# Sixteen modulation vectors of layer 1, computed in the FFN's down stage and not in layer 0's last attention heads

## The chip, the cores and the metric

The kernel runs on one core of one Trainium2 chip. The metric is the device time of one execution in microseconds (us), as a median over several runs. The core has five engines that run side by side: TensorE (PE, with its weight loads as PEld), VectorE (DVE), ScalarE (ACT), GpSimd (POOL) and SyncE (SP, which here only issues transfers). They wait for each other by semaphores.

## What is computed

The reference is a network of two layers over 512 latent tokens and 256 context tokens of width 1024. Layer 0 mixes tokens by multi-head latent attention with 8 heads, layer 1 by a gated linear recurrence with 8 heads. A SwiGLU FFN of width 2816 follows each. Every sub-layer is normalised and then shifted, scaled and gated by modulation vectors:

```
def modulate(x, shift, scale):
    return x * (1 + scale) + shift

def swiglu(a, w1, w3, w2):
    return (jax.nn.silu(a @ w1) * (a @ w3)) @ w2
```

The modulation is a product of SiLU(c), for the latent and for the context tokens, with a weight matrix of each layer: 48 vectors of 128 values a layer. In the kernel four of them make a group, named here by its first vector; groups 0, 4, 8 and 12 of layer 1 hold the shift and scale of its first norm.

## The kernel before

All arithmetic is float32. Where accuracy counts, a value is split into a high and a low part, and a product takes three matmuls: high by high, high by low, low by high (`mm3`, L96 to L102, rows L100, L101 and L102 of the trace). A weight tile is loaded to a buffer `wf`, ScalarE casts its high part (`wh` or `sh`) and VectorE or GpSimd subtracts the low part (`wl`, `sl`).

The program is written once in program order. A scheduler then sets the order of each engine's instructions, with priorities for named pieces of work (`PRIO`); the piece `ada_m` has the priority −500, so its instructions fill places that the others leave.

**The modulation.** `ada(l, u0, n, pool, bank)` (L153 to L171) computes n vectors of layer l from vector u0 on. For each it takes a buffer of the ring and lets SP load 512 KB of weights into it (L158), and TensorE runs eight matmuls of 32 columns (L161):

```
w = self.ring.tile([P, RING], F32, tag="wf", name="adaw", bufs=4)
nc.sync.dma_start(out=w[:, :D], in_=self.a["ADA"][l, u0 + i])
```

A group of four is so 32 matmuls (each is two instructions in the trace), one copy of the result by ScalarE (`rows`, L164), four transposes by TensorE (L167), and a small reduction and an addition by VectorE (L169, L171). The ring with the tag `wf` has four buffers, and all weight loads of the program share them, in program order.

**The attention heads.** `mla_attend` (from L430) runs the eight heads of layer 0. A head projects its queries, keys and values with a weight WUP, then runs six blocks of queries: the scores of one block (L517 to L521), the maximum (L524), the exponential (L527), six transposes (L533), and the values for each pair of blocks. Behind each head stand the groups that the table `ADA_HEAD` gives for it (L544), where numbers from 48 on are layer 1's. Behind the heads come three column tiles of the out-projection, with the weight MWO.

**The FFN's down stage.** `ffn_down_first` (L739) multiplies by W2 with Strassen's scheme: seven products in the place of eight. The inner dimension goes in three chunks (`CHUNKS`) of 4, 4 and 3 tiles. Each chunk has four turns (c = 0 to 3), and each turn two column tiles of the result. A turn loads two pieces of W2 (L748), forms sums of them (`sa`, `sb`) and their high and low parts, runs seven products of 12 matmuls with 384 columns (84 in the first two chunks), and adds the results to the residual. In a chunk's last turn the operands of the next chunk are loaded (`d`, L735, from ScalarE's queue) and split (`op`). The text names the four turns of the second chunk B, C, D and E. TensorE's results go to banks named `L` (two), `M` (one) and `q` (five); `self.big` hands out L, L, M in rotation.

Behind layer 0's FFN `norm_scale(1, 0)` (L312) reads the sums of groups 0 to 12.

Of the kernel before, what the change touches and what calls it, by code (L numbers as in the profile page):

```python
# [41 lines left out]
BC_LEN = 1024  # L42
RING = 1024
BT = 3
ADA_HEAD = ((), (16,), (20,), (), (24,), (28,), (32, 36), (48, 52, 56, 60))
ADA_HG = ((), (), (), (), (), (), (), (24, 28, 32))
ADA_O = (36,)
KEEP, CUTS, SB, GSB = (0, 11), (0, 2), (4, 4), (0, 9)
# [10 lines left out]
class Kernel:  # L59
# [370 lines left out]
    def mla_attend(self, es):  # L430
# [10 lines left out]
        for h in range(H):  # L441
# [61 lines left out]
            with self.at("m_att" if h < H - 1 else "m_last"):  # L503
                for q0, nq, k0, k1 in ((0, 2, 0, TT), (2, 2, 0, TT), (4, 2, 4, TT)):
# [37 lines left out]
                    else:  # L542
                        self.split(os[h][0][:, qs], os[h][1][:, qs], ov, nc.vector)
            for u in ADA_HEAD[h]:  # L544
                with self.at("ada_m"):
# [193 lines left out]
    def ffn_down_first(self, l, x, segs, hn, ops, gd, fs, ps, ft, st, spool, acc):  # L739
        nc = self.nc  # L740
        for ci, (p0, p1) in enumerate(CHUNKS):
            m = p1 - p0
            last = ci == len(CHUNKS) - 1
            for c in range(KD // 2):
                raw = []
                for k in (c, c + KD // 2):
                    w = self.ring.tile([P, RING], F32, tag="wf", name="wf", bufs=4)
                    nc.sync.dma_start(out=w[:, :2 * m * P], in_=self.a["W2"][l, k, :, 2 * p0 * P:2 * p1 * P])  # L748
                    raw.append(w)
                after = None  # L750
                if c == KD // 2 - 1 and not last:
                    after = lambda t: self.down_operand(t, gd[ci + 1], ops, ft)
                y = st()
                self.strassen(raw, m * P, y, ops[:m], fs, ps, DOWN_DVE, after)
                yv = y.rearrange("p a b -> p (a b)").rearrange("p (a b) -> p a b", a=2)
                for i, k in enumerate((c, c + KD // 2)):
                    self.residual(x, k, [yv[:, i, c0:c1] for _, c0, c1 in segs], self.mod[l][:, 40 + k, :], segs,
                                  spool if last else None, acc if last else None)
# [433 lines left out]
```

## Time and profile before

| | us |
|---|---|
| median of three runs | 1838.24 (1836.86 to 1839.51) |
| the profiled execution | 1838.41 |
| its span, first to last instruction | 1836.3 |
| mean granted clock of TensorE, full speed is 1 | 0.978 |

A profile shows one execution. The busy share of an engine is the time in which it has an instruction, over the span. In a timeline row the columns are start, duration, engine, line, operation, result and inputs with their shape, and the number of instructions; a bracket holds the idle time of the engine just before and what ended it. A row of waits holds the engine and line that waited, what it waited for, the sum in us, how often, and the longest. Where instructions of an engine overlap in a pipeline, the distance of two starts is the cost, not the duration.

### The profile page before, as it was taken

The numbers are of one execution on the slowest core, as the hardware profiler recorded it, in microseconds if no ns is written. First come the engines' busy times: TensorE is split into PE (matmuls) and PEld (weight loads), VectorE is DVE, ScalarE is ACT, GpSimd is POOL, SyncE is SP. The second block draws the span as 40 slices with busy tenths as digits, with TensorE's granted clock in tenths as the row PEclk, the third lists the DMA queues.
The fourth block names the chain that finished last, engine by engine and source line by source line (L and its number), as shares of the span: only waits on it lengthen the run. The fifth ranks groups of instructions, "written<-read, shape, count | busy, mean of one in ns | idle before, by whom it ended". The sixth has DMA issues, their size and how long they took to land. (4 is left out here: it accounts for less than half of the span.)

```text
span 1836.3 us, 33260 instructions
## 1 busy us (share of the span) xinstructions
PE 1740.9 (95%) x13576; PEld 1594.1 (87%) x13576; DVE 1186.0 (65%) x1916; ACT 815.6 (44%) x1597; POOL 705.0 (38%) x496
## 2 busy tenths in 40 slices
PE   4989999999899999999998999999998889999999
PEld 3878988778799999999996888888886779999888
DVE  5566897741765656598897666575745278888400
ACT  4455565532544444454454332433333265555411
POOL 2343342216566666620004554555543440000442
PEclk9999999999999999999997999999999999999999
DMA  8411032423233433364434121111115333333331
GB/s 274 134 49 65 24 117 98 170 77 122 104 115 126 146 123 121 113 198 146 147 119 163 47 69 48 60 57 59 59 36 196 103 128 114 97 112 104 112 116 49
DMA packets 64391, 198.14 MB, mean 108 GB/s; under 512 B 6640, under 2 KB 18800, under 8 KB 64240
## 3 DMA queue, kind: packets, MB, share of 16 engines
q1 hardware_dynamic: 61216, 180.90, 29.7%
q10 hardware_dynamic: 3024, 15.14, 2.6%
q8 instruction: 106, 1.74, 0.4%
q14 instruction: 45, 0.37, 0.1%
HBM read 178.77 MB, written 17.24 MB: 107 GB/s over the span
## 5 line engine op out<-in xcount | busy, mean ns | idle before, releaser
L87 POOL TENSOR_TENSOR wl<-wf,wh 128x1024 fp32r<-128x1024 f32 (+3 forms) x98 | 228.4, 2337 | 346.7 <-ACT wh L86 339.5
L100 PE MATMUL q<-op,sh 128*128 128x384 f32 (+1 forms) x816 | 257.1, 317 | 4.8 <-ACT op L631 2.5
L101 PE MATMUL q<-op,sh 128*128 128x384 f32 (+1 forms) x816 | 256.9, 316 | 0.0
L102 PE MATMUL q<-op,sl 128*128 128x384 f32 (+1 forms) x816 | 254.2, 317 | 0.5 <-DVE sl L626 0.5
L86 ACT CAST wh<-wf 128x1024 fp32r<-128x1024 f32 (+3 forms) x98 | 97.9, 1001 | 165.1 <-PE L L101 78.0
L100 PEld LDWEIGHTS q<-op,sh 128*128 128x128 f32 x816 | 153.8, 189 | 6.8 <-ACT op L631 3.1
L101 PEld LDWEIGHTS q<-op,sh 128*128 128x128 f32 x816 | 153.8, 189 | 0.0
L102 PEld LDWEIGHTS q<-op,sl 128*128 128x128 f32 x816 | 152.9, 188 | 0.8 <-DVE sl L626 0.8
L625 ACT CAST sh<-wf 128x1024 fp32r<-128x1024 f32 (+1 forms) x104 | 85.5, 823 | 86.5 <-PE L L101 37.2
L100 PE MATMUL L<-op,sh 128*128 128x384 f32 (+1 forms) x368 | 118.2, 321 | 3.0 <-ACT sh L625 3.0
L197 POOL TENSOR_TENSOR acc<-acc,sq 128x512 f32<-128x512 f32 (+1 forms) x30 | 35.3, 1177 | 218.2 <-ACT sq L193 218.2
L102 PE MATMUL L<-op,sl 128*128 128x384 f32 (+1 forms) x368 | 117.8, 320 | 0.1
L101 PE MATMUL L<-op,sh 128*128 128x384 f32 (+1 forms) x368 | 117.7, 320 | 0.0
L626 POOL TENSOR_TENSOR sl<-wf,sh 128x1024 fp32r<-128x1024 f32 (+1 forms) x40 | 90.3, 2258 | 61.2 <-ACT sh L625 61.2
L1121 DVE TENSOR_TENSOR X<-X,T 128x512 f32<-128x512 f32 x96 | 78.2, 856 | 48.9 <-PE lv L1046 45.4
L625 ACT CAST sh<-sb 128x1024 fp32r<-128x1024 f32 (+1 forms) x52 | 53.7, 1033 | 95.4 <-PE q L101 51.5
L100 PE MATMUL L<-f_hi,wh 128*128 128x512 f32 (+1 forms) x232 | 86.3, 372 | 0.0
L101 PE MATMUL L<-f_lo,wh 128*128 128x512 f32 (+1 forms) x232 | 85.8, 370 | 0.0
L102 PE MATMUL L<-f_hi,wl 128*128 128x512 f32 (+1 forms) x232 | 85.4, 368 | 0.0
L625 ACT CAST sh<-sa 128x1024 fp32r<-128x1024 f32 (+1 forms) x52 | 53.7, 1034 | 54.6 <-PE q L101 39.8
L100 PE MATMUL M<-op,sh 128*128 128x384 f32 (+1 forms) x244 | 75.9, 311 | 0.0
L102 PE MATMUL M<-op,sl 128*128 128x384 f32 (+1 forms) x244 | 75.7, 310 | 0.0
(475 smaller groups left out, 5364.1 us busy)
## 6 DMA issues: line engine op xcount, KB each, us to landing
wf<-in_W SPq DMA_DIRECT2D x120, 512.0 KB, 3.6
adaw<-in_ADA SPq DMA_DIRECT2D x96, 512.0 KB, 4.4
wf<-in_HW SPq DMA_DIRECT2D x32, 512.0 KB, 3.5
d<-gd ACTq DMA_DIRECT2D x14, 768.0 KB, 5.2
gd<-s SPq DMA_DIRECT2D x11, 768.0 KB, 4.3
wf<-in_W SPq DMA_DIRECT2D x16, 384.0 KB, 3.2
gd<-s SPq DMA_DIRECT2D x11, 384.0 KB, 2.8
wf<-in_MWO SPq DMA_DIRECT2D x8, 512.0 KB, 4.3
```

The source lines that it names most:

```text
L86: nc.scalar.copy(hi[:, :n], w[:, :n])
L87: nc.gpsimd.tensor_sub(lo[:, :n], w[:, :n], hi[:, :n].bitcast(F32))
L100: nc.tensor.matmul(out, lhsT=lh, rhs=rh, start=(new and i == 0), stop=False, skip_group_check=more)
L101: nc.tensor.matmul(out, lhsT=lh, rhs=rl, start=False, stop=False, skip_group_check=more)
L102: nc.tensor.matmul(out, lhsT=ll, rhs=rh, start=False, stop=(i == n - 1), skip_group_check=more)
L197: (eng or nc.gpsimd).tensor_add(acc[:, c0:c1], acc[:, c0:c1], sq[:, :n])
L625: nc.scalar.copy(hi[:, :n], s)
L626: (nc.vector if j in on_dve else nc.gpsimd).tensor_sub(lo[:, :n], s, hi[:, :n].bitcast(F32))
L1121: nc.vector.tensor_tensor(v, v, t, op=ALU.mult)
```

## The change

Layer 1's groups 0, 4, 8 and 12 (48 to 60 in the table) leave the list of the last head. They are computed in the four turns of the down stage's second chunk, one group a turn, after the turn's Strassen products in program order, with no priority of their own (the name `ada_m` is not used there) and with `self.big` for their banks. In the table group 36 of layer 0, which stood behind head 6 with group 32, moves behind the last head.

```
-ADA_HEAD = ((), (16,), (20,), (), (24,), (28,), (32, 36), (48, 52, 56, 60))
+ADA_HEAD = ((), (16,), (20,), (), (24,), (28,), (32,), (36,))
+ADA_DOWN = (0, 4, 8, 12)
...
                 self.strassen(raw, m * P, y, ops[:m], fs, ps, DOWN_DVE, after)
                 yv = y.rearrange("p a b -> p (a b)").rearrange("p (a b) -> p a b", a=2)
+                if ci == 1:
+                    self.ada(1, ADA_DOWN[c], 4, fs, self.big)
```

What it moves on the engines is seen in the order of their instructions. Each row is a line of the program, the operation, its result and inputs, the shape and how many stand in a row. In the changed kernel lines have numbers higher by one, behind L756 by three; here by one.

ScalarE in head 5, where the norm of the next head's projections ends (`lg`, `y`) and the copy of a group stands (`rows`). Before:

```order
L527 ACTIVATE p,rsum<-sc,nm 128x768
L242 ACTIVATE lg<-ss,eps 128x9
L244 ACTIVATE y<-lg 128x9
L164 COPY rows<-L 128x512
L493 CAST qk_hi<-M 128x3x128
L541 COPY oT<-ov 128x256
L535 CAST pt_hi<-tp_3505 128x6x128
L527 ACTIVATE p,rsum<-sc,nm 128x768
L86 CAST wh<-wf 128x512
```

And after:

```order
L528 ACTIVATE p,rsum<-sc,nm 128x768
L243 ACTIVATE lg<-ss,eps 128x9
L87 CAST wh<-wf 128x512
L245 ACTIVATE y<-lg 128x9
L165 COPY rows<-L 128x512
L494 CAST qk_hi<-M 128x3x128
L542 COPY oT<-ov 128x256
L536 CAST pt_hi<-tp_3505 128x6x128
L528 ACTIVATE p,rsum<-sc,nm 128x768
```

The cast of the 512-column WUP weight has moved ahead, from behind the second exponential to ahead of `y`.

SP in the down stage, with the stores of the up stage's last result and then the loads of W2. Before:

```order
L748 DMA wf<-in_W 128x1024
L728 DMA gd_5438<-s 128x4x384
L748 DMA wf<-in_W 128x1024 x9
L748 DMA wf<-in_W 128x768 x8
L85 DMA wf<-in_HW 128x1024 x2
```

And after:

```order
L749 DMA wf<-in_W 128x1024 x3
L159 DMA adaw<-in_ADA 128x1024 x4
L749 DMA wf<-in_W 128x1024 x2
L159 DMA adaw<-in_ADA 128x1024 x4
L749 DMA wf<-in_W 128x1024 x2
L159 DMA adaw<-in_ADA 128x1024 x4
L749 DMA wf<-in_W 128x1024 x2
L159 DMA adaw<-in_ADA 128x1024 x4
L749 DMA wf<-in_W 128x768 x8
```

Between the two loads of one turn and those of the next stand now four loads of modulation weights.

TensorE at the end of turn D, with the last products of the turn (`q`) and the first of turn E behind them. Before:

```order
L100 MATMUL q<-op_5453,sh 128x384
L101 MATMUL q<-op_5453,sh 128x384
L102 MATMUL q<-op_5453,sl 128x384
L100 MATMUL L<-op_5450,sh 128x384
L101 MATMUL L<-op_5450,sh 128x384
L100 MATMUL q<-op_5450,sh 128x384
L101 MATMUL q<-op_5450,sh 128x384
```

And after:

```order
L101 MATMUL q<-op_5249,sh 128x384
L102 MATMUL q<-op_5249,sh 128x384
L103 MATMUL q<-op_5249,sl 128x384
L162 MATMUL M<-adaw,s_79 32x128 x27
L168 MATMUL L<-ident,rows 128x128 x4
L101 MATMUL L<-op_5246,sh 128x384
L102 MATMUL L<-op_5246,sh 128x384
L101 MATMUL q<-op_5246,sh 128x384
L102 MATMUL q<-op_5246,sh 128x384
L103 MATMUL L<-op_5246,sl 128x384
```

27 of the group's 32 matmuls and its transposes stand in one piece between the two turns.

## Rows read from the trace of the kernel before

**Rows 1.** The page, part 1: busy us of each engine, share, instructions.
```profile
PE 1740.9 (95%) x13576; PEld 1594.1 (87%) x13576; DVE 1186.0 (65%) x1916; ACT 815.6 (44%) x1597; POOL 705.0 (38%) x496
```

**Rows 2.** Window: length, PE, PEld, DVE, ACT, POOL, PEclk, DMA share, GB/s.
```profile
860.00:880.00 20.00, 19.92 (x114) 19.60 (x112) 20.00 (x37) 14.16 (x29) 0.00 (x0) 1.00 0.53 176
```

**Rows 3.** Timeline of PE, a later stage with modulation fragments among matmuls.
```profile
974.34 0.34 PE L102 MATMUL M<-op,sl 128*128 128x384 f32 x1
974.61 0.62 PE L161 MATMUL L<-adaw,s 128*32 128x128 f32 x10
...
975.44 0.34 PE L101 MATMUL L<-op,sh 128*128 128x384 f32 x1
...
977.03 0.34 PE L101 MATMUL q<-op,sh 128*128 128x384 f32 x1
977.29 0.42 PE L161 MATMUL L<-adaw,s 128*32 128x128 f32 x6
...
977.92 0.34 PE L101 MATMUL M<-op,sh 128*128 128x384 f32 x1
```

**Rows 4.** Waits of PE from 301 to 395 us: total, times, longest.
```profile
PE L L161 <- DMA adaw<-in_ADA: 1.0, 1, 1.0
PE sc L517 <- ACT p L527: 0.5, 1, 0.5
PE L L167 <- ACT rows L164: 0.4, 1, 0.4
PE L L100 <- DVE v_lo L470: 0.3, 1, 0.3
PE ov L101 <- DVE pt_lo L536: 0.2, 1, 0.2
```

**Rows 5.** DMA issues from 225 to 365 us: number, KB, us to landing.
```profile
wf<-in_MWO SPq DMA_DIRECT2D x4, 512.0 KB, 4.8
wf<-in_WUP SPq DMA_DIRECT2D x2, 256.0 KB, 2.9
```

**Rows 6.** Timelines of SP and ACT in head 5.
```profile
305.09 2.84 SPq L158 DMA_DIRECT2D adaw<-in_ADA  x4
306.25 0.21 ACT L244 ACTIVATE y<-lg 128x9 f32<-128x9 f32 x1
306.88 0.59 ACT L164 COPY rows<-L 128x512 f32<-128x512 f32 x1 [0.42 <-PE L L161]
```

**Rows 7.** The page, part 6: landing of a W2 load.
```profile
wf<-in_W SPq DMA_DIRECT2D x120, 512.0 KB, 3.6
```

**Rows 8.** Timelines of ACT and DVE in the down stage: a weight's high and low part.
```profile
898.57 1.05 ACT L625 CAST sh<-wf 128x1024 fp32r<-128x1024 f32 x1 [1.10 <-PE M L101]
899.65 1.23 DVE L626 TENSOR_TENSOR sl<-wf,sh 128x1024 fp32r<-128x1024 f32 x1
```

**Rows 9.** Timelines of PE, DVE and ACT in the last head.
```profile
390.54 0.39 PE L517 MATMUL sc<-qk_hi 128*128 128x512 f32 x1
392.46 0.96 DVE L524 TENSOR_REDUCE nm<-sc 128x1 f32<-128x768 f32 x1 [1.99 <-PE sc L521]
393.46 0.90 ACT L527 ACTIVATE p<-sc,nm 128x768 f32<-128x768 f32 x1 [3.97 <-DVE nm L524]
396.94 0.38 PE L517 MATMUL sc<-qk_hi 128*128 128x256 f32 x1 [1.11 <-ACT p L527]
```

**Rows 10.** Waits of SP's queue from 830 to 960 us.
```profile
SPq L748 <- DVE sl L626: 94.5, 13, 13.9
```

**Rows 11.** Waits of all engines from 860 to 945 us.
```profile
ACT op L631 <- DMA d<-gd: 12.0, 8, 4.0
...
PE L L100 <- ACT sh L625: 1.2, 2, 1.0
...
PE q L100 <- ACT op L631: 1.0, 1, 1.0
...
PE q L100 <- ACT s L830: 0.7, 1, 0.7
```

## The prediction

> **What bounds the kernel now.** I read five views, in this order: the engines' shares, the windows by stage, TensorE's waits in the two stretches that the change touches, the timelines there, and the DMA landings. The first shows PE busy for 95% of the span [rows 1], so the time is PE's own work plus the little it waits. The second asks what stands beside PE where work arrives. In the down stage PE is busy for 19.92 of 20 us and VectorE for 20.00 of 20 [rows 2]: there is no hole to fill, and 114 matmuls in 19.92 us make 0.175 us each, so one turn of 84 matmuls takes 14.7 us. In the heads the change takes work away from a chain (score, maximum, exponential, transposes, values) that has its own length. So the question is: how much of the work's time do the heads give back once it is gone, and does the down stage take all of it on top? My numbers stand in lines of the kernel before; the changed file is one line longer from L45 on, three from L757 on.
>
> The profiled execution took 1838.41 us, with a span of 1836.3 and 2.1 outside it, which the change doesn't touch. It lies 0.17 us above the median of the three runs (1838.24), so I add to it directly.
>
> **What the moved work costs PE.** One group is 32 program matmuls of 32 columns (64 in the trace), whose weights are a quarter of the array high, then four transposes. The scheduler cuts a group into fragments between other matmuls. Three rows of the same kind, in a later stage, price a fragment [rows 3]. From the last 384-column matmul ahead of the x10 fragment (974.34) to the second one behind (975.44) are 1.10 us; two matmuls are 0.35, so the fragment costs 0.75. The x6 one costs 977.92 − 977.03 − 0.35 = 0.54. The four instructions more, which begin one more set of eight, make 0.21 to 0.22. So I price a fragment at 0.32 plus 0.222 for each set of up to eight trace instructions. The order of the kernel before has the four groups in 18 fragments with 39 sets, which is 5.8 + 8.7 = 14.4 us. The changed order has them in 20 fragments with 39 sets, 6.4 + 8.7 = 15.1 us. The 16 transposes cost the same in both places and are left out. Group 36, which ran in five fragments of 9 sets, becomes one of 8 in the head after: 4 × 0.32 + 0.22 = 1.5 us less.
>
> **What the heads give back.** Removed: 14.4 + 1.5 = 15.9. The PE waits of 301 to 395 us sum to 2.4 [rows 4]; they come from the old places and I let them all go. New idle time stands against these 18.3:
> (a) ScalarE. In the changed order the cast of the 512-column WUP weight stands ahead of `y` (L244), which the next head's transposes follow. SP no longer issues the x4 of 305.09 for group 36 there, and the WUP load takes the place of the first of them. Landed in 2.9 [rows 5], cast in about 0.6 (ScalarE's copy of the rows, of the same size, took 0.59 [rows 6]), it is ready at 308.6, where `y` began at 306.25. So the chain is 2.3 late, and nothing else stands ready for PE: 2.3.
> (b) The first out-projection weight. Its buffer is released only by group 36's matmuls, which now run in the head after. From these to the first matmul that wants it PE has about 3.0 us of work. The landing is between the 3.6 of a W2 load [rows 7] and the 4.8 that these took among the old ada loads [rows 5]; I take 4.0, nearer the free one, and the 1.05 cast [rows 8]: 2.0. Three weight casts now stand ahead of an exponential on ScalarE, which wait with it: 1.1 more. Together 3.1.
> (c) The scores. A score's buffer is free once the exponential of the one before has read it. From the score at 390.54 its maximum begins at 392.46, the exponential at 393.46 for 0.90: about 4.0 us from score to score, and where less work stands between, PE waits (1.11 at 396.94) [rows 9]. In the changed order of the last two heads three pairs have only 2.1, 3.2 and 3.1 us of matmuls between them, which the fill used to make up: 1.9 + 0.8 + 0.9 = 3.6.
> Sum of the new idle time 9.0, so the heads give back 18.3 − 9.0 = 9.3 us. Bounds: if none of (a) to (c) shows, 18.3; if each is half as large again and the old waits stay, 15.9 − 13.5 = 2.4. I take the middle, because each comes from a row of the same chain.
>
> **What the down stage takes.** The four turns B to E of the second chunk (from 868 on) each get one group.
> Its PE time: 15.1, all of it on the path, since PE there has next to no idle time. From below: if the 0.32 of a switch is hidden there, 8.7.
> ScalarE's copy of the rows stands between the last matmul and the transposes: 0.59 [rows 6]. In turn D nothing is left to cover it, because all 27 remaining matmuls and the transposes close the turn: 0.7. In the other turns matmuls of the turn cover it, and without these each would cost the same 0.7.
> SP's queue. The four ada loads are queued between one turn's W2 loads and the next's, in one ring of four buffers. SP waited 94.5 us in 13 waits for these buffers before [rows 10], which means the W2 loads came as early as the ring allows, two turns ahead. With four more buffers used in each turn they come one turn ahead. Behind each waiting ada load stands the next turn's W2. In turns B, C and E its buffers come free early enough. In D they come free inside the burst of 27: behind the third of these matmuls stand 24, 1.33 us, then transposes 0.44, the copy 0.7, and four matmuls of the next turn 0.7 before the first that needs the low half: 3.2 us. The load needs 3.6 to land, the cast 1.05, the low half 1.23 [rows 7, 8]: 5.9. So PE waits 2.7 in turn E. From below 0, if the buffer is released before the burst; from above 5.9.
> What the old waits give: 1.0 and the larger part of 1.2 in turn B, where PE waited for a cast and an operand, now have ada matmuls to run: −2.0. The 0.7 of the stage's end goes the same way [rows 11]: −0.7.
> VectorE and ScalarE get four small reductions, additions and copies, under 4 us in all, beside their 20.00 of 20; I cost them at nothing, because PE is what the turn waits for; if VectorE became the bound it would be 1.5.
> Sum: 15.1 + 0.7 + 2.7 − 2.0 − 0.7 = 15.8 (bounds 8.7 − 2.7 = 6 and 15.1 + 2.8 + 5.9 = 23.8). Behind it norm_scale of layer 2 reads the groups' sums; group 12 ends in turn E, with the four turns of the third chunk still to come, so nobody waits for it.
>
> **Net.** Unrounded, 15.76 − 9.32 = +6.4: 1838.41 + 6.4 = 1844.8 us.
>
> **The rivals.**
> *Moved one for one.* Terms (a) and (c) may not show: the scheduler's order is one thing, and a chain that is 2.3 late in one head may have slack before its next matmul. Then the heads give 18.3 − 3.1 = 15.2 against 15.8: +0.6, 1839.0 us. For it speaks that the visible waits of this stretch are small (2.4 in 94 us), against it that they are small because the fill was there. It needs PE's idle time in 301 to 407 to stay under about 7.
> *Faster.* The W2 loads are in time, the copy is covered, and the heads give all: 15.1 − 2.7 − 18.3 = −5.9, 1832.5 us. It needs the down stage to take the groups without a single new wait. Against it stands the one turn's lead that is lost.
> *The transfers collide.* 16 loads of 512 KB come into 85 us in which ScalarE already waited 12.0 us, in 8 waits, for the operands d [rows 11]. If the third chunk's operands, asked for in turn E, stand behind two ada loads of 3.6 us each, they land 7.2 later, and PE's next turn starts some 6.6 later: +13, 1851.4 us. It decides from the point where an operand is later than the turn it is for; the ones of before were landed with some us to spare.
> The Trainium skill (DMA: Bandwidth & Descriptors, section Issuing engines are not separate DMA queues) says that transfers started by different engines run on the same 16 DMA engines and interleave. By that rule d, which ScalarE's queue starts, is not spared by SP's ada loads, which is this rival; the trace of before has no ada load beside a d to show it.
> *The change does nothing.* It can't be: the orders differ at all places named.
>
> **How the numbers follow.** The forecast, +6.4, has 0.57; moved one for one 0.22; the collision 0.11; faster 0.10. About 0.2%, 3.7 us, is what a measurement of this kernel can tell from no change. The forecast and the collision lie beyond it: slower 0.68. Moved one for one lies within: same 0.22. Faster 0.10. The forecast's own range, with its terms' bounds not all at one end, is +3 to +12. The range of 8 in 10 reaches from within the one-for-one case (−2.4) to the collision (+13.6): 1836 to 1852; it leaves out the faster case and the worst of the bounds.
>
> **What would show it.** Of the changed kernel: PE from the first score of head 5 to the out-projection's first matmul 9 us shorter; a wait of about 2 us for a cast of the first MWO weight, and waits of score for exponential summing to some 4; turns B to E longer by 3.5 to 4.5 each, E by the 2.7 more, with a PE wait for a cast of `sh` at its start. Wrong would be: a heads stretch shorter by 15, or one not shorter at all; a turn E without a wait; operands d that land later than PE wants them; or a granted clock under 1.00 in either stretch, for which I have no term.

## The result: 1.04% slower, three times the loss that was forecast

The changed kernel takes 1859.30 us as a median of 4 runs (1855.29 to 1860.58), the kernel before 1838.88 (4 runs). The ratio is 1.0104, with a 95% interval of 1.0085 to 1.0122. A later measurement, beside 25 other runs of the kernel before, gave 1.0106 (1.0052 to 1.0160). Forecast was +6.4 us; it became about +20, outside the range. The sign was right, the size was not.

The profiled execution took 1859.18 us, with a span of 1857.2 and a clock of 0.980. Of the page, part 1 (busy us, share, instructions), against [rows 1]:

```profile
PE 1744.1 (94%) x13576; PEld 1594.3 (86%) x13576; DVE 1189.9 (64%) x1916; ACT 814.9 (44%) x1597; POOL 704.5 (38%) x496
```

The matmuls are the same in number and 3.2 us longer in sum (1740.9 before), while the span grew by 20.9: some 18 us more are idle time of TensorE. Where they lie is seen by laying the two traces side by side, matmul by matmul, without those of the groups (11,944 in each kernel):

| stretch | before, us | changed kernel |
|---|---|---|
| head 5's first score to the last block of scores in the last head | 95.5 | −1.0 |
| turn B's first matmul to the last of the third chunk | 111.1 | +21.6 |
| from there over the next 112 matmuls, to 1023 us | 40.4 | −4.0 |
| layer 1, from there to the end | 813 | +3.5 |

The missing 0.8 lies ahead of head 5 (its first score is at 302.29, before at 301.45 us), where nothing is changed. A second trace of the changed kernel, taken with the later measurement, has −1.7, +21.3, −3.5 and +4.1. So the heads, from which 16 us of work were taken by my price, gave back 1 us; the down stage, to which it was moved, grew by 21.6, of which 4.0 come back right behind it. The waits of PE in the heads, from 301 to 407 us (total, times, longest):

```profile
PE sc L518 <- ACT p L528: 4.7, 5, 1.7
PE M L493 <- DVE qk_hi L496: 2.7, 2, 1.9
PE M L493 <- POOL arena L264: 2.0, 1, 2.0
PE M L493 <- DVE arena L484: 1.4, 1, 1.4
PE ov L101 <- ACT pt_hi L536: 1.3, 2, 0.9
PE tp L534 <- DVE pt_lo L537: 1.0, 1, 1.0
PE ov L102 <- DVE pt_lo L537: 0.6, 1, 0.6
PE L L101 <- DVE adas L170: 0.6, 1, 0.6
PE L L168 <- ACT rows L165: 0.5, 1, 0.5
PE L L101 <- ACT oa L632: 0.2, 1, 0.2
```

They sum to 15.0 where they were 5.7 before (2.4 of them up to 395 [rows 4]). And TensorE's clock, which was 1.00 in this whole stretch before, falls. Windows of the changed kernel (columns as in [rows 2]):

```profile
310.00:315.00 5.00, 2.79 (x23) 2.31 (x21) 4.53 (x8) 2.05 (x6) 3.40 (x5) 0.96 0.94 373
315.00:320.00 5.00, 4.72 (x17) 4.24 (x18) 2.94 (x8) 1.75 (x6) 1.00 (x1) 0.50 0.00 0
320.00:325.00 5.00, 5.00 (x33) 4.68 (x32) 4.08 (x10) 3.86 (x10) 0.00 (x0) 0.86 0.00 0
335.00:340.00 5.00, 2.38 (x12) 1.85 (x13) 5.00 (x8) 3.64 (x6) 4.92 (x5) 0.85 0.70 282
340.00:345.00 5.00, 5.00 (x29) 4.55 (x28) 4.96 (x8) 2.67 (x8) 5.00 (x3) 0.81 0.43 118
```

From 310 to 315 PE was busy for 2.79 of 5 us, because the transposes `M` waited 1.9 us for VectorE (`qk_hi`), behind the late norm, and a matmul after them 0.6. In the next 5 us the granted clock is 0.50, the 1.2 GHz level, and PE does 17 matmuls in 4.72 us. The Trainium skill (TensorE: Matmul & The Clock Gate, section on HAM oscillation) says that waits between runs of matmuls bring the clock down, so that the next run starts slowly; this row agrees, and the experiments below show that it is not so each time.

In the down stage the timeline of PE at the end of turn D shows the step that the prediction named:

```profile
928.52 1.73 PE L162 MATMUL M<-adaw,s 128*32 128x128 f32 x54
931.00 0.66 PE L168 MATMUL L<-ident,rows 128*128 128x128 f32 x4 [0.75 <-ACT rows L165]
934.30 0.44 PE L101 MATMUL L<-op,sh 128*128 128x384 f32 x1 [2.65 <-ACT sh L626]
```

SP issues the two W2 loads of turn E only inside this burst, and ScalarE's cast waits for them:

```profile
928.99 0.81 SPq L749 DMA_DIRECT2D wf<-in_W  x2
```

```profile
933.21 1.04 ACT L626 CAST sh<-wf 128x1024 fp32r<-128x1024 f32 x1 [2.26 <-DMA wf<-in_W]
```

What follows was not in the prediction. Windows of the changed kernel:

```profile
925.00:930.00 5.00, 5.00 (x75) 4.72 (x73) 3.29 (x6) 0.48 (x1) 0.00 (x0) 1.00 0.03 4
930.00:935.00 5.00, 1.60 (x18) 1.07 (x8) 1.75 (x5) 1.63 (x2) 0.00 (x0) 1.00 0.99 359
935.00:940.00 5.00, 4.71 (x18) 4.44 (x17) 4.80 (x9) 3.00 (x6) 0.00 (x0) 0.66 0.22 69
```

PE was busy for 1.60 of 5 us, then the clock is at 0.66 for 5 us. And the first turn of the third chunk has a late weight too; the waits of PE from 925 to 965:

```profile
PE L L101 <- ACT sh L626: 2.6, 1, 2.6
PE q L103 <- DVE sl L627: 1.7, 1, 1.7
PE L L168 <- ACT rows L165: 0.8, 1, 0.8
PE L L103 <- DVE sl L627: 0.3, 1, 0.3
```

### The profile page after: what moved, and what is told of

It reads as the page before. It is cut to its first block, busy times and chain, and to the rows that moved or that the text cites. A ratio compares the mean times of both kernels' runs of the same rounds, so it can differ in the third digit from the quotient of the medians.

```text
span 1857.2 us, 33265 instructions
## 1 busy us (share of the span) xinstructions
PE 1744.1 (94%) x13576; PEld 1594.3 (86%) x13576; DVE 1189.9 (64%) x1916; ACT 814.9 (44%) x1597; POOL 704.5 (38%) x496
## 5 line engine op out<-in xcount | busy, mean ns | idle before, releaser
L101 PE MATMUL L<-op,sh 128*128 128x384 f32 (+1 forms) x422 | 135.0, 321 | 5.1 <-ACT sh L626 5.1
L103 PE MATMUL L<-op,sl 128*128 128x384 f32 (+1 forms) x422 | 134.3, 319 | 0.3 <-DVE sl L627 0.3
L102 PE MATMUL L<-op,sh 128*128 128x384 f32 (+1 forms) x422 | 134.1, 319 | 0.0
L101 PEld LDWEIGHTS L<-op,sh 128*128 128x128 f32 x422 | 79.7, 189 | 7.2 <-ACT sh L626 6.6
L103 PEld LDWEIGHTS L<-op,sl 128*128 128x128 f32 x422 | 79.8, 189 | 1.0 <-DVE sl L627 0.6
L102 PEld LDWEIGHTS L<-op,sh 128*128 128x128 f32 x422 | 80.0, 190 | 0.0
L101 PE MATMUL L<-f_hi,wh 128*128 128x512 f32 (+1 forms) x232 | 79.6, 343 | 0.0
L102 PE MATMUL L<-f_lo,wh 128*128 128x512 f32 (+1 forms) x232 | 79.5, 343 | 0.0
L103 PE MATMUL L<-f_hi,wl 128*128 128x512 f32 (+1 forms) x232 | 79.0, 341 | 0.0
```

The lines of the kernel that those rows point to most:

```text
L101: nc.tensor.matmul(out, lhsT=lh, rhs=rh, start=(new and i == 0), stop=False, skip_group_check=more)
L102: nc.tensor.matmul(out, lhsT=lh, rhs=rl, start=False, stop=False, skip_group_check=more)
L103: nc.tensor.matmul(out, lhsT=ll, rhs=rh, start=False, stop=(i == n - 1), skip_group_check=more)
```

## The experiments

The theories: A, the heads are a chain of waits in which the groups ran almost for nothing; B, the prediction's, 9 us come back there. A1 and A2: group 36's place matters, or it doesn't. For the down stage A is the late W2 and what it draws behind it, and C that this is not what costs: the buffers are too few in any order, or the work costs its time wherever it stands. The ratios are to runs of the kernel before on the same chip, whose medians were 1840.3 to 1841.4, and are not simply the ratios of the medians; single runs scatter there by 0.4 to 0.6% either way, so a difference under 0.2% is none. All stretches named are as in the table above.

**The heads alone, and group 36 back in it.** The four groups are left out altogether and their sums stay zero; the down stage is that of before.

```diff
+        nc.vector.memset(self.mod[1][:, 0:16, :], 0.0)
...
-                if ci == 1:
-                    self.ada(1, ADA_DOWN[c], 4, fs, self.big)
```

> The heads of the changed kernel with the four groups of layer 1 left out altogether (their sums stay zero, the down stage is as before). It prices what the heads give back when the work is gone. Theory A, from the changed kernel's trace (out-projection starts at 407.1 there, 407.3 before): the heads are a chain of waits and the groups ran in it almost for nothing, so leaving them out gives 0 to 3 us, 1836 to 1839. Theory B, the prediction's: 9 us are given back, 1829 to 1830.

Measured: 1841.40 against 1840.69, ratio 1.0005 (0.9989 to 1.0021). The same time, though four groups are gone and group 36 stands in fewer fragments, 16 us of TensorE's work by the prediction's price. The heads' stretch is 94.6 us, 0.9 less than before, with a clock of 0.95 and 14.5 us of waits: those of the changed kernel. This rules out B.

The second kernel is the same with group 36 where it was:

```diff
-ADA_HEAD = (..., (28,), (32,), (36,))
+ADA_HEAD = (..., (28,), (32, 36), ())
```

> As the heads alone (four groups left out, down stage as before), with group 36 back behind head 6. The difference to the heads alone is group 36's place with nothing else changed. Theory A1: 6 to 10 us faster than the heads alone, 1828 to 1832. Theory A2: the same within 2 us, 1836 to 1839. Theory B expects about 5 us from it (its terms a and b), 1824 to 1826.

Measured: 1835.32, ratio 0.9981 (0.9962 to 1.0000); the heads' stretch is 91.4, 4.0 less than before, at a clock of 0.98. Its first and last score:

```profile
301.60 0.50 PE L519 MATMUL sc<-qk_hi 128*128 128x512 f32 x1
```

```profile
393.05 0.38 PE L519 MATMUL sc<-qk_hi 128*128 128x256 f32 x1 [1.11 <-ACT p L529]
```

So even with the old order the four groups were worth 4 us in the heads, not 9. Between A1 (6 to 10 more) and A2 (2 at most): against the heads alone 3 us in the trace, 0.24% or 4.4 us by the ratios, 6.1 by the medians. The intervals of the two ratios overlap, so the size of group 36's part is not settled.

**Group 36 back, in the changed kernel itself.** The same edit of the table.

> The changed kernel with group 36 of layer 0 back behind head 6 (32, 36) and the last head's list empty. Theory A1: the move of group 36 delays the norm of head 6 (`y` behind the WUP cast, out to 310.0 from 306.3) and GpSimd's part behind it, and TensorE's clock falls in that wait; with it back the heads give 6 to 10 us more, 1849 to 1853. Theory A2: without the four groups the chain has the same length wherever group 36 stands: 1857 to 1860.

Measured: 1854.71, ratio 1.0098 (1.0064 to 1.0132), between A1 and A2, and not to be told from the changed kernel by the ratio. In its trace the heads' stretch is 92.0, 3.5 less than before, and the down stage +21.1.

**The down stage alone.** The groups stay in the heads and are computed a second time in the down stage.

```diff
-ADA_HEAD = (..., (28,), (32,), (36,))
+ADA_HEAD = (..., (28,), (32, 36), (48, 52, 56, 60))
 ADA_DOWN = (0, 4, 8, 12)
```

> The kernel before with all its groups in the heads, and the four groups computed once more in the down stage, as in the changed kernel. It prices the down stage alone. Theory A: +17 to +21 us (the changed kernel's turns B to F are 22 longer, of which about 4 come back behind them), 1856 to 1860, with the wait for `sh` at turn E. Theory B, the prediction's sum: +15.8, 1854 to 1855.

Measured: 1863.38, ratio 1.0129 (1.0097 to 1.0161). Down stage +21.9, then −5.2. Nearly all of the change's price is here. Leaving the groups in the heads as well costs only some 4 us more than the changed kernel (1.0129 against 1.0104 and 1.0106, with intervals that overlap), which says the same of the heads as the runs above.

**W2 first.** Each group's loads are written behind the W2 loads of the next turn, so that on SP the two W2 loads stand ahead of the four.

```diff
                     raw.append(w)
+                if (ci, c) in ((1, 1), (1, 2), (1, 3), (2, 0)):
+                    self.ada(1, ADA_DOWN[(c - 1) % 4], 4, fs, self.big)
...
-                if ci == 1:
-                    self.ada(1, ADA_DOWN[c], 4, fs, self.big)
```

> The changed kernel, with each group's loads written behind the two W2 loads of the next turn (SP: W2 of turn c+1, then the four ada loads of turn c). Theory A: the W2 of turn E is late because it is queued behind ada loads that wait for buffers; PE then waits some 4 us (with the copy ahead), its clock falls to half level for 3 us and the next W2 is late as well. With W2 first these 6 to 8 us go: 1851 to 1853. Theory C: the four buffers are simply too few, and the wait moves to the ada loads: no gain, 1858 to 1861.

Measured: 1854.29, ratio 1.0068 (1.0043 to 1.0093). The down stage is +13.5, 8.1 less than in the changed kernel. In this kernel's timelines SP issues turn E's W2 some 10 us ahead of its first cast, the cast waits for PE and no longer for the load, and PE goes from group to matmuls and back without a wait:

```profile
907.40 0.81 SPq L749 DMA_DIRECT2D wf<-in_W  x2
```

```profile
917.04 1.05 ACT L626 CAST sh<-wf 128x1024 fp32r<-128x1024 f32 x1 [1.49 <-PE q L102]
```

```profile
924.70 1.52 PE L162 MATMUL M<-adaw,s 128*32 128x128 f32 x48
926.43 0.34 PE L101 MATMUL q<-op,sh 128*128 128x384 f32 x1
...
928.02 0.60 PE L168 MATMUL L<-ident,rows 128*128 128x128 f32 x4
928.37 0.42 PE L101 MATMUL L<-op,sh 128*128 128x384 f32 x1
```

```profile
919.00:937.00 18.00, 18.00 (x156) 17.06 (x155) 14.06 (x28) 9.31 (x17) 0.00 (x0) 1.00 0.68 238
```

PE is busy for all of these 18 us and the clock stays at 1.00. So the late W2 with what it draws behind it is gone, and C's "no gain" is out. But the 8.1 are not its price alone: the order of the loads also changes the scheduler's fragments. The changed kernel has the groups in 23 pieces that cost 15.2 us (the distance of the matmuls around them, less the usual 0.175 and the stall), this one in 17 that cost 12.3, and one of them waits 1.7 us for its own weights. What is left, 13.5, is mostly PE's work for the groups: PE's waits from 866 to 960 us sum to 3.9 here, and to 2.9 before. A ring with more than four buffers was not tried.

**Two vectors a turn, in eight turns.**

```diff
-                if ci == 1:
-                    self.ada(1, ADA_DOWN[c], 4, fs, self.big)
+                if ci >= 1:
+                    self.ada(1, 8 * (ci - 1) + 2 * c, 2, fs, self.big)
```

> The changed kernel, with two vectors a turn in the eight turns of the second and third chunk, where it has four in the four turns of the second. Theory A: half as many ring buffers between two turns' W2, so the late W2 of turn E goes (6 to 8 us less), against about 3 us for four more copies and more fragments: 1854 to 1857. Theory C: the work costs PE its time wherever it stands and the waits are a small part: 1859 to 1863.

Measured: 1844.10, ratio 1.0021 (1.0000 to 1.0042), the best of the kernels with the groups in the down stage; that stage is +12.9. The time is better than both ranges. But part of it is luck: in this profiled execution the heads took 90.7 us, 4.8 less than before, at a clock of 1.00. Up to the down stage its instructions stand in the order of the changed kernel, so it was run once more.

> The kernel with two vectors a turn once more. Up to the down stage its instructions stand in the order of the changed kernel, but its heads ran at a clock of 1.00 and 4.7 us shorter than before, those of the changed kernel at 0.95 and 1.0 shorter. If the clock is the cause and falls by chance of the moment, this run shows 0.95 and about 1; if the kernel's own spacing decides, it shows 1.00 and 4 to 5 again.

Measured: 1849.28, one run. The clock of the heads is 0.95 now and the stretch 94.6 long. The first and last score of the one and then of the other:

```profile
300.25 0.50 PE L518 MATMUL sc<-qk_hi 128*128 128x512 f32 x1
...
390.96 0.38 PE L518 MATMUL sc<-qk_hi 128*128 128x256 f32 x1 [1.11 <-ACT p L528]
```

```profile
301.23 0.50 PE L518 MATMUL sc<-qk_hi 128*128 128x512 f32 x1
...
395.83 0.39 PE L518 MATMUL sc<-qk_hi 128*128 128x256 f32 x1 [1.11 <-ACT p L528]
```

And the windows, of the first and then of the second execution:

```profile
310.00:315.00 5.00, 2.66 (x16) 1.92 (x15) 4.89 (x10) 1.65 (x6) 2.82 (x5) 1.00 0.49 195
315.00:320.00 5.00, 5.00 (x38) 4.63 (x37) 4.68 (x12) 3.73 (x10) 0.00 (x0) 1.00 0.00 0
```

```profile
310.00:315.00 5.00, 2.51 (x16) 1.88 (x15) 4.75 (x10) 1.90 (x4) 3.58 (x6) 0.86 0.55 198
315.00:320.00 5.00, 5.00 (x20) 4.52 (x20) 2.81 (x7) 1.47 (x7) 0.08 (x1) 0.50 0.00 0
```

One kernel, the same waits in sum (14.9 us in both), PE busy for 2.66 and 2.51 us of the five ahead: once the clock stays, and PE does 38 matmuls in the next 5 us, once it falls to half and PE does 20. The difference in the stretch, 94.60 − 90.71 = 3.9 us, is the price of the clock in the heads; 0.946 over 94.6 us is 10.2 us at the half level. Seven profiled executions have this order of the heads (the changed kernel twice, the heads alone, W2 first, the rotation set back, and these two); six have the clock of 0.95, and stretches of 93.6 to 94.6 us, so the price is 2.9 to 3.9.

**The banks' rotation.** `self.big` gives L, L, M in turn, and eight calls more shift it for the rest of the program.

```diff
+                    k = self.nbig
                     self.ada(1, ADA_DOWN[c], 4, fs, self.big)
+                    self.nbig = k
```

> The changed kernel, with the rotation of the banks L, L, M set back behind each group, so that the rest of the program has the banks of the kernel before. Behind the down stage (980 to 1020) the changed kernel gets 4 to 5 us back, and in layer 1 it loses 3. Theory R: both come from the shifted rotation; with it undone the return is gone, 1862 to 1865, less what layer 1 gives back. Theory S: the return comes from transfers and clock behind a later start; time as the changed kernel, 1858 to 1861.

Measured: 1850.43, ratio 1.0045 (1.0028 to 1.0061), neither theory's number. In the trace the down stage is +16.2, 5.4 less than with the shifted rotation, since the scheduler places the fragments otherwise (from turn D's last product to turn E's are 23.4 us at a clock of 1.00, where the changed kernel needs 25.9 at 0.93), and only 2.6 come back behind it. In layer 1 it is 1.7 us faster than before, the changed kernel 3.5 slower. R fails for the larger part of the return: 3.8 us come back ahead of the norm's first transposes here too (3.5 in the changed kernel). What is less lies behind them, where the clock is 0.84 from 1007.2 to 1039.2 us and the changed kernel's is 0.95 from 1011.2 to 1041.6. The medians of the two kernels differ by some 9 us, their traces by 7.4; how much of this the banks decide and how much the clock is open.

**The two parts together, and both orders.** Two vectors a turn, W2 first, and two vectors W2 first (from the first chunk's last turn on), each with group 36 back.

> Two vectors a turn in eight turns, and group 36 back behind head 6: both parts that the runs so far point to. Two vectors a turn alone gave +4 us against the kernel before, group 36's place 4 to 5 us in the heads alone. Theory: the two add, 0 us, 1839 to 1842 beside 1841 of the kernel before. Rival: they do not add, since the heads end where their chain ends, +4, 1844 to 1846.

> Each group's loads behind the turn's own W2 loads, four vectors a turn, and group 36 back behind head 6. W2 first alone gave +12 to +13 us. Theory: less 4 to 5 for group 36, +8, 1848 to 1850. Rival: +12, 1852 to 1854.

> Two vectors a turn, each pair's loads behind the turn's own W2 loads, from the last turn of the first chunk on, and group 36 back behind head 6. Theory A: no W2 is late any more, what is left is PE's work for the groups (14 to 15 us less 4 for old waits) against 5 us in the heads and 3 to 5 behind the stage: 0 to +3, 1840 to 1844. Rival: as much is lost to more fragments as is won, +5 to +8.

Measured: 1846.60, ratio 1.0032 (1.0004 to 1.0061), the rival's side; 1851.22, ratio 1.0049 (1.0016 to 1.0082), between both; 1852.92, ratio 1.0064 (1.0036 to 1.0093), worse than its rival. The down stage is +11.9, +12.9 and +18.0, counted in the last from the first chunk's third turn, where its first fragments stand. The gains do not add. No order of the groups in the down stage brought it much under +12.

The changed kernel stood beside them:

> The changed kernel as it is, beside the others on one chip. +18 to +21 against the kernel before, 1859 to 1862 if that stands at 1841.

Measured: 1859.84, ratio 1.0106 (1.0052 to 1.0160), as expected.

**Groups in other heads, and more of them.** First two of the four groups in heads 0 and 3.

```diff
-ADA_HEAD = ((), (16,), (20,), (), (24,), (28,), (32, 36), (48, 52, 56, 60))
+ADA_HEAD = ((48,), (16,), (20,), (52,), (24,), (28,), (32, 36), (56, 60))
```

> The kernel before, with the groups 0 and 4 of layer 1 moved to heads 0 and 3, whose lists are empty, and 8 and 12 left in the last head. Theory A: the heads take groups almost for nothing (four cost 4 to 5 us there against 17 us of PE's work), and the last head with its own waits is not better at it than others: 1836 to 1840 on the chip of the first runs, no more than 0.2% either way. Theory D: heads 0 and 3 are bound by PE and each group costs its full 4.2 us there: 1843 to 1847.

Measured: 1839.65, ratio 0.9996 (0.9979 to 1.0014). No difference, theory A. Then two groups more, 16 and 20 of layer 1, taken from the norm behind the FFN: behind the last head (`(48, 52, 56, 60, 64, 68)`), or behind heads 0 and 3; and three more, 24, 28 and 32, from layer 1's last head:

> The kernel before, with two more groups of layer 1 (16 and 20) in the last head's list, taken from the norm behind the FFN, where the clock is at 0.67 from 980 to 1000. Theory A, the heads hide groups almost for nothing: the stretch grows by 1 to 3 us for the two, and the norm behind the FFN is shorter by up to their 8 us: 1835 to 1839 where before stands at 1841. Theory B, each group costs its PE time in the heads too: 0 to +3, 1841 to 1844.

> The same two groups, in heads 0 and 3, whose lists are empty. Theory A: 1835 to 1839, if these heads hide them as the last does. Theory B: their full price in the heads, 1841 to 1845.

> As the one before, and the groups 24, 28 and 32 of layer 1 moved from layer 1's last head to the last head of layer 0, which then has seven. Theory A: nearly nothing in the heads, less what layer 1's head hid anyway: 1833 to 1840. Theory B: three groups at 4 us in the heads against the same in layer 1: 1841 to 1850.

Measured: 1848.61, ratio 1.0025 (1.0008 to 1.0041); 1846.19, ratio 1.0036 (1.0018 to 1.0054); 1854.27, ratio 1.0073 (1.0053 to 1.0094). The stretch in the first is 98.3 us, 2.8 more than before for two groups more, or 1.4 each where PE's work for one is some 4: in the last heads A holds for these too, which is what was open. All heads together, first score of head 0 to the last, grow by 5.9 in the second, 3.0 a group, and by 10.0 in the third, 2.0 a group. That the whole kernel got slower lies behind the heads. The norm behind the FFN did not get shorter by the two groups taken from it: in the first its transposes start 12.4 us behind the stage's last product, where they started 10.5 behind it, because TensorE now waits for the norm's sums:

```profile
991.62 1.68 PE L208 MATMUL q<-ident,acc 128*128 128x128 f32 x6 [12.04 <-DVE acc L195]
```

At 1023 us this kernel was 2.1 us ahead of the kernel before and at the end 6.0 behind it; of these 8 us in layer 1 6.4 lie in two stretches in which its clock was lower (0.92 where before had 0.94, 0.99 where before had 1.00). None of these beats the kernel before.

## Why the prediction was wrong, step by step

**What the heads give back: 9.3 predicted, 1.0 measured.** This is the step that failed most: 8.3 of the 14.5 us by which the profiled execution misses the sum (20.9 against 6.4), where the down stage has 5.8, less the 4.0 that come back, layer 1 has 3.5 and the start 0.8. Its parts, with the execution of this order at full clock (90.71, 4.8 less than before) and those at 0.95:

- The work removed was sized too high. At full clock the stretch is 4.8 shorter with 9.2 us more of waits, so 14.0 of PE's time went, not the 15.9; and the 14.0 have the 16 transposes in them, which the prediction left out on both sides.
- The waits were sized too low. Net of the old ones I had 9.0 − 2.4 = 6.6; they rose from 5.7 to 15.0, by 9.3. Of the three mechanisms named, (a) and (c) show. For (a), ScalarE's timeline after:

```profile
309.49 0.62 ACT L87 CAST wh<-wf 128x512 fp32r<-128x512 f32 x1 [2.44 <-DMA wf<-in_WUP]
310.02 0.20 ACT L245 ACTIVATE y<-lg 128x9 f32<-128x9 f32 x1
```

  `y` is 7.7 us behind head 5's first score (302.29), where it was 4.8 behind it before (306.25 − 301.45): 2.9 late, and 2.3 were predicted. The transposes `M` behind it waited 1.9. But waits of `M` for VectorE and GpSimd sum to 6.1 of the 15.0, and the other 4.2 (at 334, 339 and 361 us) stand in the norms of the later heads, where the prediction had nothing. For (b) no wait for the weight's cast shows; PE waited for `arena` there. For (c) the score's waits for the exponential are 4.7 in five places.
- The clock had no term. It cost some 3.9 us. The prediction named a clock under 1.00 as what would make it wrong, but looked at no row for how a stretch fares in which PE is idle for a seventh of the time; the trace of before had one, 980 to 1000 us, with PE busy for 14.38 of 20 and a clock of 0.67.

9.3 − 1.9 − 2.7 − 3.9 = 0.8, and 1.0 was seen.

**What the down stage takes: 15.8 predicted, 21.6 measured, 17.6 with what comes back behind it.** From the distances of the matmuls from turn B to the end of the third chunk: the groups' fragments cost 15.2 us (predicted 15.1, there without the transposes). The stall at turn E was right in place and size: 0.75 for the copy and 2.65 for W2, against 0.7 and 2.7. Old gaps of 4.9 are gone and others of 1.8 came in turns B, C and E, 3.1 net, where 2.7 were predicted. Three things had no term. The half clock behind the stall made turn E's other matmuls 2.1 us longer. The turn after had a late W2 of its own, 2.1. And the matmuls behind a fragment are a little slower, 1.7 in all. Together 5.9, against a difference of 5.8. The late W2 with the half clock and the second late W2 makes 2.65 + 2.1 + 2.1 = 6.9 in this trace, and W2 first, in which all three are gone, takes 8.1 off with fewer fragments; so this term was right as a cause and sized at two fifths.

The 4.0 that come back behind the stage were not predicted either. Of them 3.5 lie between the stage's last product and the first transposes of the norm behind it, 10.5 us before and 7.0 after. VectorE's sum and TensorE's rows, before and then after:

```profile
990.02 0.69 DVE L195 SCALAR_TENSOR_TENSOR acc<-acc,sq 128x512 f32<-128x512 f32 x1 [1.92 <-ACT sq L193]
992.22 1.08 PE L161 MATMUL M<-adaw,s 128*32 128x128 f32 x16 [0.23 <-DMA adaw<-in_ADA]
993.23 1.54 PE L208 MATMUL q<-ident,acc 128*128 128x128 f32 x6
```

```profile
1010.40 0.69 DVE L196 SCALAR_TENSOR_TENSOR acc<-acc,sq 128x512 f32<-128x512 f32 x1 [0.53 <-ACT sq L194]
1011.23 1.12 PE L209 MATMUL q<-ident,acc 128*128 128x128 f32 x4
1012.27 1.08 PE L162 MATMUL L<-adaw,s 128*32 128x128 f32 x16
```

Before, 98 modulation instructions stand between the last product and the transposes, with 3.1 us of waits for their loads, and the transposes start 2.5 us behind the end of the first sum they read. In the changed kernel 64 stand there and 32 behind, and they start 0.1 us behind it. The other 1.1 is the sum itself, which ends 6.9 us behind the last product and not 8.0; why is open. The clock is not it: it is 0.69 in this gap before and 0.72 after.

```profile
983.10:993.20 10.10, 6.27 (x102) 3.71 (x102) 5.35 (x8) 3.06 (x6) 4.60 (x6) 0.69 0.84 303
1004.60:1011.20 6.60, 4.07 (x68) 2.65 (x68) 5.51 (x8) 2.17 (x6) 4.11 (x5) 0.72 0.91 337
```

The part ahead of the transposes comes back in all kernels with groups in the down stage (2.3 to 3.9 us) and in none without.

**Rivals.** "Moved one for one" needed the idle time of 301 to 407 to stay under about 7; it is 15. "The transfers collide": the loads `d` were not late, ScalarE waited 4.1 us for them from 866 to 960 where it had been 12.0 [rows 11]; PE waited for W2. "Faster" needed all W2 in time. The time came out where none of the rivals stood, since all of them varied one side at a time and none had the clock.

**Left over.** Layer 1 is 3.5 us longer in the changed kernel's trace. It is also 4.0 longer with the heads alone, where nothing of layer 1 is changed but its start, and 6.7 with group 36 back in them. Part of it is the clock. The last 165 us of the kernel before ran at a clock of 1.00, and so they did in six other traces, within 0.5 us of its time; in nine, the changed kernel's two among them, the clock there is 0.99 and they are 1.4 to 2.0 us longer (1.6 in the changed kernel), and in two, at 0.98, 2.8 and 2.9. Of the rest 1.7 lies from 1386 to 1549 us, where the changed kernel's clock was no lower than before (0.95 and 0.94) and its second trace is 0.3 shorter than before; what it is stays open, and so does what the shifted rotation has to do with it.

## What to carry to other kernels

Work that fills a chain of waits is worth in time only what it prolongs the chain, and that is measured by leaving it out, not by its own length: here 14 to 16 us of work were worth 1 to 5. When fill is taken away, price the idle time twice, as a wait and as the clock behind it. When loads are added to a ring that another load uses, look at which load stands behind them on the queue; to write them behind it is one line, and was worth 8 us of the stage here, some 3 of them by fewer fragments. And lay several traces of one kernel side by side before a difference of 2 or 3 us in one of them is given a cause.

## What was not expected of the hardware

The same kernel in the same order, with PE busy for 2.5 to 2.7 of 5 us, kept its clock once at 1.00 and lost half of it another time; the difference was 3.9 us in 95. The last wait ahead of the fall, of the transposes `M` for `qk_hi`, was 1.75 us in the execution that kept its clock and 1.86 to 1.91 in the six that lost it; whether this decides it, no run shows. And the fall comes behind a single stall as well: 1.60 of 5 us busy, then 0.66 for 5 us. The Trainium skill (TensorE: Matmul & The Clock Gate, section on HAM oscillation) tells of a clock that swings with the waits at each tile; why it falls in six executions of seven in the same order with nearly equal waits, and stays in the other, no run here explains.
